# A Macaron encoder block on one core: output products in another order, an output projection by frame tile, norms without GpSimd

## The chip, the cores and the metric

The kernel runs on 1 core of one Trainium2 chip. The metric is the device time of one execution in microseconds, lower is better. A run gives one time; the figure used is the median of several runs of the same kernel.

## The reference

One streaming-encoder layer on 1024 frames of 1024 features, float32, with 256 memory tokens. `rms` is an RMS norm with a gain per feature.

```python
x  = x + 0.5 * rms(swiglu(rms(x, f1pre), ffn1_in, ffn1_out), f1post)   # D_FF 2816
h  = rms(x, mixpre)
q, k, v, g_out, f_low, p_in, xq, gates = split(h @ w_in)
a  = gated linear attention over 64-frame chunks (q, k, v, decay from f_low)
b  = trailing means of 2, 4, 8, 16 frames of p_in, a linear map per group
c  = cross-attention of xq into the normed memory
merged = sigmoid(gates) . (a @ w_up_gla, b @ w_up_pool, c @ w_up_xattn)
x  = x + rms(merged @ w_o, mixpost)
x  = x + 0.5 * rms(swiglu(rms(x, f2pre), ffn2_in, ffn2_out), f2post)
return rms(x, final_g)
```

## The kernel before, in words

**Tiles.** The frames are cut into 8 tiles of 128 (`NT`; `TPH` = 4 of them are a half). A matmul takes a 128x128 weight and 512 moving columns. For float32 accuracy each operand is split into a high and a low part (`acopy` on ScalarE writes the high one, `low` on VectorE subtracts it from the full one), and each product is three matmuls: low by high, high by low, high by high. Big arrays stand in 46 buffers of 128x1024 (`NB`, pool `bp`), all given out in one queue by first use; PSUM has 8 banks.

**Stages in order of time.** First norm and transposes; `ffn` for the first feed-forward part; its outputs are finished tile by tile by `finish1` (L923), which also makes the next norm and, by `turn2`, transposes the tile on TensorE; then keys, values, projections, attention, pooling and the three up-projections; then the output projection (L1385 to L1400); `ffn` again, finished by `finish2` and `last_norm` (L1408 on), which write the output.

**The output products of `ffn`** (L719 to L751). The second matrix product of the feed-forward part, 1024 frames by 2816 by 1024, is done with seven products of half size in place of eight (`out_product`, numbered 0 to 6). Each takes 11 steps of m, 4 frame tiles and 3 matmuls: 132 matmuls into 4 banks. By `by_rows` = 0 the steps run outermost, so all 4 tiles end together; by 2, two tiles are run through before the other two; by 1, tile after tile (33 matmuls each). The order before is 0, 4, 1, 5, 3, 2, 6. Product 2 completes frame tiles 0 to 3 and product 6 tiles 4 to 7, and each completed tile goes to `finish`.

**A norm** is `post_norm` (square and sum on ScalarE, a few 128x1 operations on VectorE for the inverse root, a product with the gain row, two `scalar_tensor_tensor` that scale and add the residual) and then `pre_norm` (the same for the next norm: product with the gain row, then a `tensor_scalar` by the inverse root). Its transposes are queued in `pending` and given out by `flush(keep)`.

**The output projection.** An outer loop over the two halves of the columns (`nh`), an inner one over the 8 tiles, 24 matmuls each; the norms of all tiles stand in the second half, after each tile's second group. `turn3` transposes a tile, splits it for tiles 0 to 3, and spills it to DRAM (`hfd`), from where `t_sums` fetches it again and forms the sums that the next `ffn` multiplies by. `between2` calls `t_sums` at j == 5 of the eight first products that `ffn` runs ahead.

**What orders the work.** Nothing is issued as it is written. A `Recorder` (class at L31) notes each operation with its engine, an estimated duration and what it depends on. `issue` (L188) then plays all of it through as a list schedule: an engine that is free takes the ready operation that was written first, a buffer is granted in the queue's order, and the sequence so found is fixed as each engine's instruction order. An operation with an `alt` may go to GpSimd (POOL) where that engine is free first: `tt` with `alt=True` (L149), used for the products with gain rows and for `low` of most weights.

```python
    def tt(self, o, a, b, op, alt=False):
        self.add("DVE", 0.07 + self.n(a) * 0.00104, [o], [a, b],
                 lambda: self.nc.vector.tensor_tensor(o, a, b, op=op),
                 alt=(0.1 + self.n(a) * 0.0022,
                      lambda: self.nc.gpsimd.tensor_tensor(o, a, b, op=op)) if alt else None)
```

In the trace all operations of one helper have one line: matmul L129, transpose L132, ScalarE's activation L146, VectorE's `tensor_tensor` L151 and its GpSimd alternative L153, `scalar_tensor_tensor` L162, `tensor_scalar` L168, `reciprocal` L171, DMA L186. So a place is told by its tiles: `ps` a PSUM bank, `b` a big buffer, `io` a residual tile, `g` a gain row, `s` the 128x1 scalars, `raw`/`wh`/`wl` a weight and its parts, `hh`/`hl` the parts of a transposed tile.

Of the kernel before, what the change touches and what calls it, by code (L numbers as in the profile page):

```python
# [35 lines left out]
class Recorder:  # L36
# [48 lines left out]
    def add(self, eng, dur, outs, ins, fn, table=None, alt=None):  # L85
# [31 lines left out]
        self.ops.append((eng, dur, deps, fn, table, alt))  # L117
# [16 lines left out]
    def act(self, o, i, func, scale=1.0, bias=0.0, accum_out=None):  # L134
# [9 lines left out]
        fixed = (0.052 if i.space == PSUM else 0.094) + (0.093 if accum_out is not None else 0.0)  # L144
# [14 lines left out]
    def stt(self, o, a, s, b, op0, op1):  # L159
        ins = [a, b] + ([] if isinstance(s, float) else [s])  # L160
        self.add("DVE", (0.07 if isinstance(s, float) else 0.13) + self.n(a) * 0.00104, [o], ins,
                 lambda: self.nc.vector.scalar_tensor_tensor(o, a, s, b, op0=op0, op1=op1))  # L162

    def ts(self, o, a, s1, s2, op0, op1=None):
        ins = [a] + [s for s in (s1, s2) if s is not None and not isinstance(s, (int, float))]
        kw = {} if op1 is None else {"op1": op1}
        self.add("DVE", (0.07 if len(ins) == 1 else 0.13) + self.n(a) * 0.00052, [o], ins,
                 lambda: self.nc.vector.tensor_scalar(o, a, s1, s2, op0=op0, **kw))  # L168

    def recip(self, o, a):  # L170
        self.add("DVE", 0.09, [o], [a], lambda: self.nc.vector.reciprocal(o, a))  # L171

    def reduce(self, o, a, axis, op):
        self.add("DVE", 0.07 + self.n(a) * 0.00105, [o], [a],
                 lambda: self.nc.vector.tensor_reduce(o, a, axis=axis, op=op))

    def vcopy(self, o, a):
        self.add("DVE", 0.07 + self.n(a) * 0.001, [o], [a], lambda: self.nc.vector.tensor_copy(o, a))

    def memset(self, o, v):  # L180
        self.add("DVE", 0.07 + self.n(o) * 0.001, [o], [], lambda: self.nc.vector.memset(o, v))
# [7 lines left out]
    def issue(self):  # L189
# [109 lines left out]
        for i in seq:  # L299
            ins = (ops[i][3] if ran[i] == ops[i][0] else ops[i][5][1])().ins  # L300
# [14 lines left out]
def block_kernel(  # L315
# [47 lines left out]
    def tt(o, a, b, op, alt=False):  # L363
        R.tt(o, a, b, op, alt)

    def low(o, full, high, alt=False):
        R.tt(o, full, high.bitcast(F32), op=ALU.subtract, alt=alt)
# [18 lines left out]
    def load_w(src, n=1024, alt=True):  # L386
# [3 lines left out]
        low(wl[:, :n], raw[:, :n], wh[:, :n], alt)  # L390
# [94 lines left out]
    def post_norm(y, gt, res, factor, table, alt=True):  # L485

        rs = row_rstd(y, factor, table)
        if alt:
            tt(y, y, gt, ALU.mult, alt=True)
        else:  # L490
            for i in range(2):
                cs = slice(i * 512, (i + 1) * 512)
                tt(y[:, cs], y[:, cs], gt[:, cs], ALU.mult)
# [111 lines left out]
    def ffn(win, wout, ops, between, finish, midway=None, ahead=6):  # L605
# [115 lines left out]
        ylo, yhi = y[:TPH], y[TPH:]  # L721
# [795 lines left out]
```

## Time and profile before

| | |
|---|---|
| median of 3 runs | 2380.36 us (2377.5 to 2385.82) |
| the profiled execution's own time | 2375.9 us |
| its span | 2374.1 us |
| mean granted TensorE clock | 0.984 |
| TensorE matmul busy | 2277.9 us, 96% |
| VectorE busy | 1556.9 us, 66% |
| ScalarE busy | 991.8 us, 42% |
| GpSimd busy | 125.1 us, 5% |

The table's busy times are over the whole span. A table by stretches of time gives for each stretch its length, the busy time of each engine with its instruction count, the granted clock and the DMA share. A list of waits says which engine's queue stood at which line, and on whose result. A timeline has one row for each instruction or run of equal ones: start, duration, engine, line, operation, output and inputs, and in brackets how long the engine had been idle and who released it. PE is TensorE, DVE VectorE, ACT ScalarE, POOL GpSimd.

### The profile page before, as it was taken

To read this page: it belongs to the slowest core of one execution; us is meant where nothing else is said; L and a number is where in the kernel's file an instruction comes from. 1 tells how busy PE (TensorE), PEld (TensorE's weight loads), DVE (VectorE), ACT (ScalarE), POOL (GpSimd) and SP (SyncE) were. 2 spreads that over 40 slices of the span, in tenths; PEclk is the share of its full clock that TensorE was granted. 3 is DMA by queue.
4 is the path that set the end of the run, shared out by engine and by line. 5 is a ranking of instruction groups with operands and counts; after the bars stand their busy time and mean duration, and the time that the engine had idled before them with its cause. 6 is when DMAs were issued, how large, how long until landed. Compare 5 with 4: busy or idle time off the path is not lost. (4 is left out here: it accounts for less than half of the span.)

```text
span 2374.1 us, 28161 instructions
## 1 busy us (share of the span) xinstructions
PE 2277.9 (96%) x10085; PEld 1843.9 (78%) x10085; DVE 1556.9 (66%) x2477; ACT 991.8 (42%) x1649; POOL 125.1 (5%) x53
## 2 busy tenths in 40 slices
PE   7999999999979999999999999999789999999996
PEld 6788888888768887777777788887668878888885
DVE  7887776754493545755666745553978877766448
ACT  7432333444356532366555542122543323345435
POOL 1000000000130002100000000001400000000002
PEclk8999999999999999999999999999999999999998
DMA  5346663676364632434444465341534666448553
GB/s 172 111 164 207 224 210 130 220 239 197 135 199 133 231 104 83 135 124 145 151 151 153 154 216 225 104 133 46 201 126 151 233 221 213 166 149 285 178 169 124
DMA packets 188477, 398.42 MB, mean 168 GB/s; under 512 B 19534, under 2 KB 50126, under 8 KB 188336
## 3 DMA queue, kind: packets, MB, share of 16 engines
q1 hardware_dynamic: 188336, 396.62, 50.0%
q8 instruction: 79, 1.29, 0.2%
q14 instruction: 62, 0.51, 0.1%
HBM read 273.34 MB, written 123.21 MB: 167 GB/s over the span
## 5 line engine op out<-in xcount | busy, mean ns | idle before, releaser
L129 PE MATMUL ps<-hl,wh 128*128 128x512 f32 (+1 forms) x1592 | 629.9, 396 | 14.7 <-ACT b L146 6.3
L129 PE MATMUL ps<-hh,wl 128*128 128x512 f32 (+1 forms) x1592 | 631.7, 397 | 6.5 <-DVE wl L151 6.5
L151 DVE TENSOR_TENSOR wl<-raw,wh 128x1024 fp32r<-128x1024 f32 x390 | 492.1, 1265 | 206.6 <-ACT wh L146 161.0
L146 ACT ACTIVATE wh<-raw 128x1024 fp32r<-128x1024 f32 x396 | 411.9, 1057 | 323.7 <-PE ps L129 150.2
L129 PE MATMUL ps<-hh,wh 128*128 128x512 f32 (+1 forms) x1592 | 427.9, 390 | 0.0
L129 PEld LDWEIGHTS ps<-hl,wh 128*128 128x128 f32 x1592 | 301.5, 189 | 91.8 <-issue 9.2
L129 PEld LDWEIGHTS ps<-hh,wl 128*128 128x128 f32 x1592 | 301.7, 190 | 68.2 <-DVE wl L151 7.8
L129 PEld LDWEIGHTS ps<-hh,wh 128*128 128x128 f32 x1592 | 299.2, 189 | 62.6 <-issue 0.7
L146 ACT ACTIVATE t<-ps 128x512 f32<-128x512 f32 x202 | 119.6, 597 | 417.3 <-PE ps L129 408.4
L129 PE MATMUL ps<-wl,wh 128*128 128x512 f32 x616 | 241.4, 392 | 4.6 <-DVE s L171 2.1
L129 PE MATMUL ps<-wh,wl 128*128 128x512 f32 x616 | 240.8, 391 | 0.0
L129 PE MATMUL ps<-wh 128*128 128x512 f32 x616 | 240.7, 391 | 0.0
L151 DVE TENSOR_TENSOR t<-ps,t 128x512 f32<-128x512 f32 x214 | 146.9, 687 | 137.5 <-PE ps L129 97.1
L146 ACT ACTIVATE b<-ps 128x512 f32<-128x512 f32 (+3 forms) x286 | 137.9, 496 | 192.6 <-PE ps L129 150.3
L129 PE MATMUL ps<-b,wh 128*128 128x512 f32 (+1 forms) x576 | 169.4, 377 | 0.0
L129 PE MATMUL ps<-hh,wq 128*128 128x512 f32 x528 | 165.7, 395 | 0.0
L153 POOL TENSOR_TENSOR b<-b,g 128x1024 f32<-128x1024 f32 x20 | 51.0, 2557 | 1967.3 <-ACT junk L146 1951.8
L151 DVE TENSOR_TENSOR raw<-raw,raw 128x512 f32<-128x512 f32 x176 | 122.6, 701 | 26.9 <-DMA raw<-in_ffn_out_dram 23.1
L129 PEld LDWEIGHTS ps<-wl,wh 128*128 128x128 f32 x616 | 116.5, 189 | 29.9 <-issue 3.3
L146 ACT ACTIVATE t<-t 128x512 f32<-128x512 f32 x98 | 61.8, 632 | 179.1 <-DVE t L151 178.9
L129 PEld LDWEIGHTS ps<-wh 128*128 128x128 f32 x616 | 116.3, 189 | 24.5
L129 PEld LDWEIGHTS ps<-wh,wl 128*128 128x128 f32 x616 | 116.4, 189 | 24.0
(104 smaller groups left out, 2635.6 us busy)
## 6 DMA issues: line engine op xcount, KB each, us to landing
raw<-in_ffn_in_dram SPq DMA_DIRECT2D x102, 512.0 KB, 4.0
raw<-actd SPq DMA_DIRECT2D x154, 256.0 KB, 3.0
actd<-b SPq DMA_DIRECT2D x88, 256.0 KB, 4.1
raw<-in_ffn_out_dram SPq DMA_DIRECT2D x44, 512.0 KB, 4.2
wsd<-raw SPq DMA_DIRECT2D x88, 256.0 KB, 2.9
raw<-wsd SPq DMA_DIRECT2D x88, 256.0 KB, 3.7
raw<-in_wfm_dram SPq DMA_DIRECT2D x44, 512.0 KB, 4.4
projd<-t SPq DMA_DIRECT2D x80, 256.0 KB, 2.8
```

The lines of the kernel that those rows point to most:

```text
L129: lambda: self.nc.tensor.matmul(o, l, r, start=first, stop=last, skip_group_check=more))
L146: lambda: self.nc.scalar.activation(o, i, func, **kw),
L151: lambda: self.nc.vector.tensor_tensor(o, a, b, op=op),
L153: lambda: self.nc.gpsimd.tensor_tensor(o, a, b, op=op)) if alt else None)
```

## The change

Six edits, in both feed-forward parts or around them:

- The GpSimd alternative is gone from `tt`, `low` and `load_w`; the ten GpSimd operations of the pooling stage (`pool_tt`) stay.
- `pre_norm` makes one `scalar_tensor_tensor` of its product and `tensor_scalar`.
- The estimated durations in the Recorder have larger fixed parts.
- The output products come in the order 0, 4, 3, 5, 2, 1, 6. Product 2 still completes tiles 0 to 3; products 1 and 6 follow. Product 0's result is copied to both halves' buffers, product 3 is read from PSUM twice and not copied, product 1 gets a bank of its own. `flush(2)` becomes `flush(1)`.
- The output projection takes one frame tile at a time: both column halves, then its norm. All 8 weight tiles of `wo` are loaded at the first tile.
- The weights of key group 0 are loaded within `finish1` at tile 4; `t_sums` of the second part is called at j == 3; `finish1` uses the square-root table for all tiles.

```diff
-    def tt(self, o, a, b, op, alt=False):
-        self.add("DVE", 0.07 + self.n(a) * 0.00104, [o], [a, b],
-                 lambda: self.nc.vector.tensor_tensor(o, a, b, op=op),
-                 alt=(0.1 + self.n(a) * 0.0022,
-                      lambda: self.nc.gpsimd.tensor_tensor(o, a, b, op=op)) if alt else None)
+    def tt(self, o, a, b, op):
+        self.add("DVE", 0.15 + self.n(a) * 0.00105, [o], [a, b],
+                 lambda: self.nc.vector.tensor_tensor(o, a, b, op=op))
...
-        self.add("DVE", (0.07 if isinstance(s, float) else 0.13) + self.n(a) * 0.00104, [o], ins,
+        self.add("DVE", 0.2 + self.n(a) * 0.00105, [o], ins,
...
-        fixed = (0.052 if i.space == PSUM else 0.094) + (0.093 if accum_out is not None else 0.0)
+        fixed = (0.17 if i.space == PSUM else 0.2) + (0.19 if accum_out is not None else 0.0)
...
     def pre_norm(src, n, gt, turn, table=False):
         rs = row_rstd(src, table=table)
-        tt(n, src, gt, ALU.mult, alt=True)
-        R.ts(n, n, rs, None, op0=ALU.mult)
+        R.stt(n, src, rs, gt, op0=ALU.mult, op1=ALU.mult)
...
         for t in range(TPH):
-            acopy(ylo[t][:, lo_], b1[t])
+            acopy(y2[t][:, lo_], b1[t])
+            acopy(y1[t][:, lo_], b1[t])
         b2 = [bank() for _ in range(TPH)]
         out_product(b2, 4, lambda m: wsd[1, m], False, 0)
         for t in range(TPH):
-            tt(yhi[t][:, hi_], b2[t], ylo[t][:, lo_], ALU.add)
-        out_product(b1, 1, lambda m: wout[2 * m + 1][:, lo_], True, 0)
-        for t in range(TPH):
-            acopy(yhi[t][:, lo_], b1[t])
-        out_product(b2, 5, lambda m: wsd[2, m], True, 0)
-        for t in range(TPH):
-            tt(ylo[t][:, hi_], b2[t], ylo[t][:, lo_], ALU.add)
+            tt(y1[t][:, hi_], b2[t], y1[t][:, lo_], ALU.add)
         b3 = [bank() for _ in range(TPH)]
         out_product(b3, 3, lambda m: wsd[0, m], False, 0)
         for t in range(TPH):
-            s5 = ttile()
-            acopy(s5, b3[t])
-            tt(ylo[t][:, hi_], ylo[t][:, hi_], s5, ALU.add)
+            tt(y1[t][:, hi_], b3[t], y1[t][:, hi_], ALU.add)
+        out_product(b2, 5, lambda m: wsd[2, m], True, 0)
+        for t in range(TPH):
+            tt(y2[t][:, hi_], b2[t], y2[t][:, lo_], ALU.add)
+            tt(y2[t][:, hi_], b3[t], y2[t][:, hi_], ALU.add)
         out_product(b2, 2, lambda m: wsd[3, m], True, 2)
         for t in range(TPH):
-            tt(ylo[t][:, lo_], b2[t], ylo[t][:, lo_], ALU.add)
-            finish(t, ylo[t])
-            flush(2)
-        out_product(b3, 6, lambda m: wout[2 * m + 1][:, hi_], True, 1)
+            tt(y2[t][:, lo_], b2[t], y2[t][:, lo_], ALU.add)
+            finish(t, y2[t])
+            flush(1)
+        b1 = [bank() for _ in range(TPH)]
+        out_product(b1, 1, lambda m: wout[2 * m + 1][:, lo_], False, 0)
         for t in range(TPH):
-            tt(yhi[t][:, hi_], b3[t], yhi[t][:, hi_], ALU.add)
-            finish(t + TPH, yhi[t])
-            flush(2)
+            tt(y1[t][:, lo_], b1[t], y1[t][:, lo_], ALU.add)
+        b3 = [bank() for _ in range(TPH)]
+        out_product(b3, 6, lambda m: wout[2 * m + 1][:, hi_], False, 1)
+        for t in range(TPH):
+            tt(y1[t][:, hi_], b3[t], y1[t][:, hi_], ALU.add)
+            finish(t + TPH, y1[t])
+            flush(1)
...
-    z = [btile() for _ in range(NT)]
-    for nh in range(2):
-        ws = [load_w(wo[nh, kk], alt=False) for kk in range(4)]
-        for t in range(NT):
-            cs = slice((t % TPH) * P, (t % TPH + 1) * P)
+    ws = {}
+    for t in range(NT):
+        z = btile()
+        cs = slice((t % TPH) * P, (t % TPH + 1) * P)
+        for nh in range(2):
+            if t == 0:
+                ws[nh] = [load_w(wo[nh, kk]) for kk in range(4)]
+            w = ws[nh]
...
     def between2(j):
         flush()
-        if j == 5:
+        if j == 3:
```

**TensorE's order at the end of the first feed-forward part.** In the fences a number behind a name is that buffer's own; `ps_608` is a bank of product 2's second pair of tiles, `b_560` and `b_561` are frame tiles 0 and 1 after their norms, and `ps_708` (before) is a bank of product 6, `ps_768` (after) one of product 1. Before:

```order
L129 MATMUL ps_608_701<-wh_780_873,wl_781_874 128x512
L129 MATMUL ps_608_701<-wh_780_873 128x512
L132 MATMUL ps_794_887<-ident_73,b_560_653 128x128 x4
L132 MATMUL ps_795_888<-ident_73,b_560_653 128x128 x4
L132 MATMUL ps_800_893<-ident_73,b_561_654 128x128 x4
L132 MATMUL ps_801_894<-ident_73,b_561_654 128x128 x4
L129 MATMUL ps_708_801<-wl_804_897,wh_803_896 128x512
```

Of the changed kernel:

```order
L129 MATMUL ps_608_701<-wh_743_836,wl_744_837 128x512
L129 MATMUL ps_608_701<-wh_743_836 128x512
L132 MATMUL ps_754_847<-ident_73,b_560_653 128x128 x4
L132 MATMUL ps_755_848<-ident_73,b_560_653 128x128 x4
L129 MATMUL ps_768_861<-wl_774_867,wh_773_866 128x512
L129 MATMUL ps_768_861<-wh_773_866,wl_774_867 128x512
```

Before, two tiles' transposes stand between product 2 and the last product; now one tile's stand there, and product 1 comes in front of product 6.

**VectorE's order for one tile of the output projection**: `io` is the residual tile, `b` the tile itself, `g` the gain row of the next norm, `s` the scalars. Before:

```order
L162 SCALAR_TENSOR_TENSOR io_2144<-b_2103,s_2145,io_2144 128x512 x2
L151 TENSOR_TENSOR b_2103<-io_2144,g_2094 128x1024
...
L168 TENSOR_SCALAR s_2146<-s_2146 128x1 x3
L168 TENSOR_SCALAR s_2149<-s_2149 128x1
L162 SCALAR_TENSOR_TENSOR s_2146<-s_2146 128x1
...
L168 TENSOR_SCALAR b_2103<-b_2103,s_2146 128x1024
```

Of the changed kernel:

```order
L151 TENSOR_TENSOR b_2107<-b_2107,g_2097 128x1024
L166 TENSOR_SCALAR s_2135<-s_2135 128x1 x2
L160 SCALAR_TENSOR_TENSOR s_2135<-s_2135 128x1 x5
...
L160 SCALAR_TENSOR_TENSOR io_2134<-b_2107,s_2135,io_2134 128x512 x2
...
L160 SCALAR_TENSOR_TENSOR b_2107<-io_2134,s_2136,g_2098 128x1024
```

The first norm's product with the gain row now stands in VectorE's queue (before it was on GpSimd's), the second norm's product and scaling are one instruction, and a tile's scalars no longer alternate with those of the next tile.

**TensorE's order at the end of the output projection**: `ps_2115`, `ps_2120`, `ps_2124` are banks of the second feed-forward part's first products; `b_2017` (before) and `b_2098` (after) are frame tile 7. Before:

```order
L132 MATMUL ps_2101_2194<-ident_73,b_2016_2109 128x128 x4
L132 MATMUL ps_2102_2195<-ident_73,b_2016_2109 128x128 x4
L129 MATMUL ps_2115_2208<-hh_2008_2101,wl_2114_2207 128x512
...
L132 MATMUL ps_2109_2202<-ident_73,b_2017_2110 128x128 x4
L132 MATMUL ps_2110_2203<-ident_73,b_2017_2110 128x128 x4
L129 MATMUL ps_2115_2208<-hh_2008_2101,wh_2113_2206 128x512
```

Of the changed kernel:

```order
L129 MATMUL ps_2124_2217<-hl_2013_2106,wh_2122_2215 128x512
L132 MATMUL ps_2113_2206<-ident_73,b_2098_2191 128x128 x4
L132 MATMUL ps_2114_2207<-ident_73,b_2098_2191 128x128 x4
L129 MATMUL ps_2124_2217<-hh_2012_2105,wl_2123_2216 128x512
```

Between the projection's last matmul and tile 7's transposes stand 62 of the next part's matmuls before and 73 now; behind the transposes, up to the first matmul that needs the sums of `t_sums`, 130 before and 119 now.

## Rows read from the trace of the kernel before

**Rows 1.** Busy time by stage: stretch, length, each engine's busy us (instructions), clock, DMA.

```profile
core 0: us, PE busy (x) PEld busy (x) DVE busy (x) ACT busy (x) POOL busy (x), PEclk, DMA share, GB/s
0.00:76.00 76.00, 57.41 (x254) 45.32 (x255) 61.68 (x150) 51.68 (x123) 7.29 (x7) 0.82 0.41 141
...
613.00:720.00 107.00, 87.91 (x373) 71.51 (x372) 87.23 (x179) 56.33 (x139) 36.91 (x14) 0.89 0.52 170
...
1650.00:1760.00 110.00, 84.31 (x383) 66.31 (x382) 95.92 (x221) 60.22 (x120) 28.36 (x10) 0.98 0.52 172
1760.00:1900.00 140.00, 140.00 (x619) 115.95 (x618) 117.27 (x167) 44.31 (x58) 0.00 (x0) 1.00 0.54 181
1900.00:1960.00 60.00, 56.65 (x240) 45.69 (x239) 47.26 (x69) 17.42 (x24) 0.00 (x0) 0.97 0.64 222
```

**Rows 2.** The same view, cut to four spells of half clock.

```profile
645.80:652.60 6.80, 4.89 (x20) 4.45 (x21) 6.33 (x15) 4.38 (x13) 2.33 (x1) 0.50 0.90 289
666.20:673.00 6.80, 5.11 (x13) 3.86 (x13) 6.33 (x13) 0.20 (x1) 0.68 (x1) 0.50 0.88 293
697.00:700.40 3.40, 2.74 (x9) 2.35 (x10) 3.22 (x11) 0.29 (x2) 0.00 (x0) 0.50 0.78 213
710.60:717.40 6.80, 5.33 (x17) 4.59 (x18) 5.73 (x20) 3.61 (x9) 0.55 (x1) 0.50 0.62 192
```

**Rows 3.** TensorE's waits, 598 to 720 us: us in total, times, longest.

```profile
PE ps L132 <- DVE s L162: 5.4, 1, 5.4
...
PE ps L132 <- DVE b L151: 2.7, 1, 2.7
PE ps L129 <- DVE s L171: 2.1, 1, 2.1
PE ps L132 <- DVE b L168: 1.9, 1, 1.9
```

**Rows 4.** GpSimd's groups by form: busy us, mean ns, idle time before.

```profile
L153 POOL TENSOR_TENSOR b<-b,g 128x1024 f32<-128x1024 f32 x20 | 51.0, 2557 | 1967.3 <-ACT junk L146 1951.8 <-DMA b<-in_x_dram 15.5
L153 POOL TENSOR_TENSOR b<-io,g 128x1024 f32<-128x1024 f32 x13 | 36.4, 2800 | 57.0 <-DVE io L162 25.2 <-issue 16.8 <-DVE s L162 12.2
L153 POOL TENSOR_TENSOR wl<-raw,wh 128x1024 fp32r<-128x1024 f32 x6 | 15.7, 2624 | 111.4 <-ACT dec L146 73.1 <-ACT wh L146 38.4
```

**Rows 5.** VectorE's groups by form, 1600 to 1760 us.

```profile
L162 DVE SCALAR_TENSOR_TENSOR s<-s 128x1 f32<-128x1 f32 x80 | 23.9, 325 | 0.6
L151 DVE TENSOR_TENSOR wl<-raw,wh 128x1024 fp32r<-128x1024 f32 x9 | 14.8, 1647 | 0.0
...
L162 DVE SCALAR_TENSOR_TENSOR io<-b,s,io 128x512 f32<-128x512 f32 x16 | 11.5, 747 | 0.3
...
L151 DVE TENSOR_TENSOR b<-io,g 128x1024 f32<-128x1024 f32 x5 | 6.1, 1225 | 0.1
```

**Rows 6.** Timeline, 1640 to 1664 us: GpSimd, then VectorE.

```profile
1649.80 2.38 POOL L153 TENSOR_TENSOR b<-b,g 128x1024 f32<-128x1024 f32 x1 [4.82 <-ACT junk L146]
...
1649.89 2.31 DVE L162 SCALAR_TENSOR_TENSOR s<-s 128x1 f32<-128x1 f32 x1
...
1652.23 0.16 DVE L162 SCALAR_TENSOR_TENSOR s<-s 128x1 f32<-128x1 f32 x1
...
1653.60 0.75 DVE L168 TENSOR_SCALAR b<-b,s 128x1024 f32<-128x1024 f32 x1
...
1657.55 0.42 DVE L151 TENSOR_TENSOR hl<-ps,hh 128x256 fp32r<-128x256 f32 x1
```

**Rows 7.** Busy time, cut at tile 7's transposes in the output projection.

```profile
1592.00:1720.30 128.30, 110.51 (x504) 90.08 (x503) 80.56 (x217) 52.80 (x123) 30.96 (x11) 0.99 0.40 135
...
1721.30:1757.70 36.40, 28.56 (x119) 21.44 (x117) 25.18 (x24) 19.28 (x27) 0.00 (x0) 1.00 0.44 140
```

**Rows 8.** Timeline at the end: TensorE's last matmul, VectorE's last two adds.

```profile
2353.07 0.39 PE L129 MATMUL ps<-wh 128*128 128x512 f32 x1
...
2354.52 0.67 DVE L151 TENSOR_TENSOR b<-ps,b 128x512 f32<-128x512 f32 x1
...
2362.32 0.69 DVE L151 TENSOR_TENSOR b<-ps,b 128x512 f32<-128x512 f32 x1
```

More of the change, by code (lines that the diff above doesn't have):

```diff
@@ L83, in _region, with add @@
         return name, m, (p0, p0 + pn)
-    def add(self, eng, dur, outs, ins, fn, table=None, alt=None):
+    def add(self, eng, dur, outs, ins, fn, table=None):
         idx = len(self.ops)
@@ L116, in add @@
         deps.discard(idx)
-        self.ops.append((eng, dur, deps, fn, table, alt))
+        self.ops.append((eng, dur, deps, fn, table))
     @staticmethod
@@ L166, in ts @@
         kw = {} if op1 is None else {"op1": op1}
-        self.add("DVE", (0.07 if len(ins) == 1 else 0.13) + self.n(a) * 0.00052, [o], ins,
+        self.add("DVE", (0.15 if len(ins) == 1 else 0.2) + self.n(a) * 0.00052, [o], ins,
                  lambda: self.nc.vector.tensor_scalar(o, a, s1, s2, op0=op0, **kw))
     def recip(self, o, a):
-        self.add("DVE", 0.09, [o], [a], lambda: self.nc.vector.reciprocal(o, a))
+        self.add("DVE", 0.15, [o], [a], lambda: self.nc.vector.reciprocal(o, a))
     def reduce(self, o, a, axis, op):
-        self.add("DVE", 0.07 + self.n(a) * 0.00105, [o], [a],
+        self.add("DVE", 0.15 + self.n(a) * 0.00105, [o], [a],
                  lambda: self.nc.vector.tensor_reduce(o, a, axis=axis, op=op))
     def vcopy(self, o, a):
-        self.add("DVE", 0.07 + self.n(a) * 0.001, [o], [a], lambda: self.nc.vector.tensor_copy(o, a))
+        self.add("DVE", 0.15 + self.n(a) * 0.001, [o], [a], lambda: self.nc.vector.tensor_copy(o, a))
     def memset(self, o, v):
-        self.add("DVE", 0.07 + self.n(o) * 0.001, [o], [], lambda: self.nc.vector.memset(o, v))
+        self.add("DVE", 0.15 + self.n(o) * 0.001, [o], [], lambda: self.nc.vector.memset(o, v))
     def dma(self, o, i):
@@ L253, in issue @@
                     i = heapq.heappop(ready[e])
-                    if ran[i]:
-                        continue
-                    dur = ops[i][1] if e == ops[i][0] else ops[i][5][0]
+                    dur = ops[i][1]
                     if ops[i][4] not in (None, table):
@@ L299, in issue @@
         for i in seq:
-            ins = (ops[i][3] if ran[i] == ops[i][0] else ops[i][5][1])().ins
+            ins = ops[i][3]().ins
             done_by[i] = ins.name
@@ L361, in acopy, with tt, low @@
             R.act(o, i, AF.Copy, scale=scale)
[L363 to L367, printed above, removed]
+    def tt(o, a, b, op):
+        R.tt(o, a, b, op)
+    def low(o, full, high):
+        R.tt(o, full, high.bitcast(F32), op=ALU.subtract)
     def mm(o, l, r, first, last, more=False):
@@ L384, in load_raw, with load_w @@
         return raw
-    def load_w(src, n=1024, alt=True):
+    def load_w(src, n=1024):
         raw = load_raw(src, n)
@@ L483, in flush, with post_norm @@
             pending.pop(0)()
-    def post_norm(y, gt, res, factor, table, alt=True):
+    def post_norm(y, gt, res, factor, table, parts=1):
         rs = row_rstd(y, factor, table)
[L488 to L493, printed above, removed]
+        for i in range(parts):
+            cs = slice(i * D // parts, (i + 1) * D // parts)
+            tt(y[:, cs], y[:, cs], gt[:, cs], ALU.mult)
         for i in range(2):
@@ L924, in into @@
             tuple(a.rearrange("p (k c) -> p k c", k=2) for a in (hh, hl)))
+    kv0 = []
     def finish1(t, yt):
@@ L931, in finish1 @@
         R.dma(xt, x[t * P:(t + 1) * P, :])
-        post_norm(yt, gains["post"], xt, 0.5, t < 6)
+        post_norm(yt, gains["post"], xt, 0.5, True)
         R.dma(x1d[t], xt)
-        pre_norm(xt, yt, gains["pre"], lambda n: turn2(n, t), t < 6)
+        pre_norm(xt, yt, gains["pre"], lambda n: turn2(n, t), True)
+        if t == TPH:
+            kv0.extend(load_w(wkv[0, kk]) for kk in range(4))
         if t >= TPH:
@@ L961, in fetch, with kv_group @@
         return b
-    def kv_group(g):
-        ws = [load_w(wkv[g, kk]) for kk in range(4)]
+    def kv_group(g, ws=None):
+        if ws is None:
+            ws = [load_w(wkv[g, kk]) for kk in range(4)]
         for pr in range(4):
@@ L1326, in side @@
         yield
-    run(chain(kv_group(0), kv_group(1)), side())
+    run(chain(kv_group(0, kv0), kv_group(1)), side())
     hops.update(B11=hm[0][0:2], B21=hm[0][2:4], B22=hm[1][2:4])
@@ L1383, in turn3 @@
         spill(f, t)
-    z = [btile() for _ in range(NT)]
-    for nh in range(2):
-        ws = [load_w(wo[nh, kk], alt=False) for kk in range(4)]
-        for t in range(NT):
-            cs = slice((t % TPH) * P, (t % TPH + 1) * P)
+    ws = {}
[6 more added lines that the diff above has]
+            w = ws[nh]
             ps = bank()
             mm3(ps, [(mh[t // TPH][k // 2][:, k % 2, cs], ml[t // TPH][k // 2][:, k % 2, cs],
-                      ws[k // 2][0][:, (k % 2) * 512:(k % 2 + 1) * 512],
-                      ws[k // 2][1][:, (k % 2) * 512:(k % 2 + 1) * 512]) for k in range(KD)])
-            acopy(z[t][:, nh * 512:(nh + 1) * 512], ps)
-            if nh == 1:
-                xt = R.tile(bp, [P, 1024], F32, "b", nm("io"), NB)
-                R.dma(xt, x1d[t])
-                post_norm(z[t], gains["mpost"], xt, 1.0, False)
-                R.dma(x2d[t], xt)
-                pre_norm(xt, z[t], gains["f2pre"], lambda n, t=t: turn3(n, t))
-                flush(1)
+                      w[k // 2][0][:, (k % 2) * 512:(k % 2 + 1) * 512],
+                      w[k // 2][1][:, (k % 2) * 512:(k % 2 + 1) * 512]) for k in range(KD)])
+            acopy(z[:, nh * 512:(nh + 1) * 512], ps)
+        xt = R.tile(bp, [P, 1024], F32, "b", nm("io"), NB)
+        R.dma(xt, x1d[t])
+        post_norm(z, gains["mpost"], xt, 1.0, False)
+        R.dma(x2d[t], xt)
+        pre_norm(xt, z, gains["f2pre"], lambda n, t=t: turn3(n, t))
+        flush(1)
     def between2(j):
         flush()
-        if j == 5:
+        if j == 3:
             t_sums(h3, True)
```

18 lines of the change are left out of this document (8 added, 10 removed).

## The prediction

> **What bounds the kernel now.** The table by stages comes first [rows 1]. Between 1760 and 1900 us TensorE is busy 140.00 of 140 us with 619 matmuls, so 0.226 us each; most of the span looks like this, and there nothing is to be had but fewer matmuls, and their number does not change. Time can go only where TensorE stands: 18.6 of 76 us at the start, 19.1 of 107 us between 613 and 720 (107 - 87.91; stage A, where the first feed-forward part ends and its tiles are normed), 25.7 of 110 us between 1650 and 1760 (stage B, the output projection and the entry into the second part), 3.4 of 60 us at 1900, and the tail behind the last matmul. Stage A pays twice: in four spells the granted clock is 0.50, so 1.2 in place of 2.4 GHz, and in each TensorE is busy only 72 to 81% of the time [rows 2]. TensorE's busy time in the four is 4.89 + 5.11 + 2.74 + 5.33 = 18.07 us; at full clock it would be half, so 9.0 us went there. Stage A lost 19.1 + 9.0 = 28.1 us.
>
> Next the list of waits [rows 3]: in stage A TensorE stands for VectorE, mostly at transposes (L132) that wait for a tile's norm. VectorE is busy 87.23 of those 107 us and 95.92 of 110 in stage B [rows 1], so it paces both, while between 1900 and 1960 it has slack. These are also the stages in which GpSimd works, 36.91 and 28.36 us. Its groups are 20 + 13 products with a gain row and 6 weight splits [rows 4], all alternatives of VectorE's work, 2.56 to 2.80 us each where VectorE takes 1.225 [rows 5]. The timeline shows what they do to VectorE [rows 6]: GpSimd starts at 1649.80 for 2.38 us, VectorE's 128x1 operation starts at 1649.89 and takes 2.31 us; the same form takes 0.16 us at 1652.23. The reader sees an instruction of one column held for as long as GpSimd runs.
>
> **The change, part by part.** *GpSimd's work goes to VectorE.* 39 instructions: 14 in stage A [rows 1], 11 in B [rows 7], 7 in the tail, 7 elsewhere. Added on VectorE at 1.225 us: 17.2 in A, 13.5 in B, 8.6 in the tail. Given back is the hold. In 1600 to 1760 us two forms show it [rows 5]: 80 one-column operations at 325 ns in place of 160 lose 13.2 us, 9 weight splits at 1647 in place of 1225 lose 3.8. That is 17.0 us of GpSimd's 30.96 [rows 7], a share of 0.55; other forms lose some too, and I take 0.6. The ends are 0.55 and 1 (all of GpSimd's time). At 0.6 stage A gets back 22.1, B 18.6.
>
> The Trainium skill, SBUF — State Buffer, section "Who interferes with whom", says that the ports are an exclusive lock: whoever comes second waits for the whole instruction. If every GpSimd instruction held VectorE so, all 36.91 us of stage A would come back, and stage A could then give all of its 28.1 us. The rows bear out the lock but not the share, since an instruction that reads PSUM ran its 0.42 us at 1657.55; I keep 0.6.
>
> *`pre_norm` as one instruction.* It removes 0.75 us (1653.60, [rows 6]) and the product of 1.225 and adds a `scalar_tensor_tensor` of 1024 columns, which no row shows. Bounds: the 1.225 of a product of that size, and two of 512 columns at 747 ns, 1.49 [rows 5]. So 0.5 to 0.75 us saved per tile, 0.6 taken: 5 us in each stage of 8 tiles. VectorE's load falls by 22.1 - 17.2 + 5 = 10 us in A and by 18.6 - 13.5 + 5 = 10 in B.
>
> *The product order, stage A.* Tiles 0 to 3 are completed before product 1 and not before the last product, so one product earlier: 132 x 0.226 = 29.9 us. Four norms and their transposes now lie beside products 1 and 6 (59.8 us of TensorE), where before they met the other four. What stays: tiles 4 to 7 still end one row of 33 matmuls (7.5 us) apart with the last product, and their transposes come last; product 1 wants banks that the first tile's transposes also want; product 6's rows need weight splits that stand among norms in VectorE's queue. I leave three of the seven waits, 2.7 + 2.1 + 1.9 = 6.7 us [rows 3], and one half-clock spell, 5.11 / 2 = 2.6 [rows 2]: 9.3 of 28.1 remain, **18.8 us gained**. The ends are 5 and 28. The second copy of product 0's result lies on ScalarE, which is busy 56.33 of 107 us here, and is costed at nothing; so is the copy of product 3 that goes. The four weight loads of key group 0 pass SP's queue earlier beside a DMA share of 0.52 [rows 1], also at nothing; uncovered they would delay weights of product 6 by a few us, which the upper end holds.
>
> *The output projection by tile, stage B.* The first matmul is at 1592.00. Up to tile 7's transposes TensorE has 384 matmuls (86.8 us), 62 of the next part (14.0), and 56 transposes of other tiles, at 0.82 us for 8 some 6 us: 106.8 us, but it takes 128.3 [rows 7], of which 17.8 are idle. Before, all norms stand in the second half of this; by tile, each norm has 48 matmuls (10.8 us) and a transpose beside it. VectorE needs for a tile some 20 scalar operations (3.5 us), 1.225 + 1.49 + 1.4 for the wide ones and 4 splits of 0.42, so about 9 us: it keeps up, if buffers come free in time. Then tile 7's transposes stand at 1592 + 106.8 + 11 x 0.226 = 1701.3, 19.0 us earlier. Behind them the chain is the same: spill, fetch, sums, first matmul on them, 36.4 us [rows 7]. Of this TensorE covers 28.56 now; with 11 matmuls fewer 26.1, so it stands 10.3 us and not 7.8. That costs no time of its own, since the chain sets the end, but one longer stand may cost a half-clock spell, again 2.6 us. **16.4 us gained**; ends 12 and 19. On SP's queue the last spill is followed by four fetches and then weight loads, where one weight load stood between; nothing is costed for that.
>
> *The tail.* The last matmul ends at 2353.46; VectorE's add of that tile's result starts at 2362.32, 8.9 us late, since the queue of earlier tiles is in front of it [rows 8]. From there 11.8 us to the span's end stay. With tiles 0 to 3 done a product earlier and no hold, the backlog has 59.8 us to vanish in; tile 6's own work (about 7 us) fits into the last row of 7.5 us. I leave one matmul's 0.4 us: **8.5 gained**, ends 5 and 9.
>
> *At nothing*: three products at the start go to VectorE, 3.7 us for 0.6 x 7.29 = 4.4 returned, beside DMA waits; the new estimated durations reorder queues where TensorE hardly stands; square roots by table for two tiles.
>
> The sum: 18.8 + 16.4 + 8.5 = 43.7 us. The profiled execution took 2375.9, so 2332.2; it lies 4.5 us under the median of 2380.36, on which the forecast is put: 2380.4 - 43.7 = **2336.7**. With all ends together the forecast's own case runs from 2324 (28 + 19 + 9) to 2358 (5 + 12 + 5); most of it lies between 2326 and 2346.
>
> **The rivals.**
> *Stage A is not gained.* Products 1 and 6 now have to share VectorE and the 8 banks with the norms; product 1 takes four banks while the transposes of tiles 0 to 3 want two at a time. For it: of the waits one stands at a matmul of a product (L129), not at a transpose [rows 3], so products are held up too. Against it: VectorE's load falls. If stage A gives 5 us: 2380.4 - 5 - 16.4 - 8.5 = 2350.5. Chance 0.12.
> *Stage B is not gained.* The 16 weight tiles of `wo`, 16 merged tiles, 8 parts of h and 2 gain rows are 42 of the 46 buffers, so tile, residual and transposed tile have four, and a tile's norm may wait for the spill of the one ahead. Then tile 7 comes when it came, 0 to 5 us gained: 2380.4 - 18.8 - 2.5 - 8.5 = 2350.6. For it: the buffers' count; against it: 17.8 us of idle time that need not be there. Chance 0.10.
> *New waits in the bodies eat the gain.* Another order of products and other durations reorder some 1,300 us in which TensorE runs without a gap. At 1900 to 1960 there is one such wait, 3.4 us and a half-clock spell that costs 1.7 (clock 0.97 of 60 us, [rows 1]). Eight of these, one at each of the four products that change place in both parts, cost 41 us: 2378, no change. Chance 0.05.
> *Slower: the hold is not GpSimd's.* If VectorE's long instructions have another cause, the 32 instructions of A, B and tail are pure load: 17.2 - 5 in A, 13.5 - 5 in B, 8.6 in the tail, 29 us on the engine that paces these stages. No order of products helps then, and 2380.4 + 29 = 2409. It decides from where less than half of the share of 0.6 comes back. Against it: [rows 6]. The Trainium skill, Perfetto Trace Analysis, section "Optimizing Scalar/DVE Operations", has the rule that work may go to GpSimd where VectorE is saturated, though the shared port may spoil it; by the first half of it this change is wrong. Chance 0.05.
> That the change does not do what it says is excluded: in the order GpSimd's queue is down to the ten operations of the pooling stage.
>
> **How the numbers follow.** The forecast has the remaining 0.68. A measurement tells about 0.3%, 7 us, from no change. Faster: 0.68 + 0.12 + 0.10 = 0.90; the same 0.05; slower 0.05. The range reaches from 2318 (all of the lower ends, and a few us more should the full hold come back) to 2360, which takes in both rivals of one stage lost; left out are the last two cases and some of the edges.
>
> **What would show it.** In the profile after: VectorE's one-column operations in stages A and B at 160 to 220 ns; no GpSimd work outside the pooling stage; TensorE idle about 7 and not 19 us at the end of the first part, tile 7's transposes about 109 us behind the projection's first matmul, then a stand of some 10 us; the last add within 1 us of the last matmul and 12 us from the end. It is wrong if TensorE waits for weight splits (`wl`) inside products 1 and 6, if the projection's matmuls wait for buffers, or if the bodies of the two parts lose more than 5 us.

## The result, and the profile after

The changed kernel takes 2312.86 us (median of 4 runs, 2312.55 to 2313.34), the kernel before 2379.96 beside it: a ratio of 0.9715 (95% interval 0.9697 to 0.9733), 67 us less. The forecast was 2336.7, in a range from 2318 to 2360; the measured time lies 5 us below that range. The profiled execution's span fell from 2374.1 to 2310.8, by 63.3 us; the profiled execution of the kernel before lies 4.1 us under its median.

The table of stretches of the changed kernel answers to [rows 1]: stage A is now 613 to 700 us, stage B 1568.4 to 1720.

```profile
0.00:76.00 76.00, 54.65 (x247) 41.49 (x247) 59.77 (x152) 52.00 (x124) 0.20 (x4) 0.86 0.39 134
...
613.00:700.00 87.00, 82.21 (x381) 67.45 (x380) 71.99 (x148) 54.05 (x123) 0.00 (x0) 0.98 0.74 239
...
1626.00:1678.30 52.30, 52.30 (x248) 43.62 (x247) 34.66 (x107) 27.22 (x59) 0.00 (x0) 1.00 0.51 168
1678.30:1720.00 41.70, 35.08 (x152) 27.21 (x151) 35.11 (x36) 26.42 (x33) 0.00 (x0) 1.00 0.41 139
...
1860.00:1960.00 100.00, 100.00 (x443) 82.81 (x442) 80.46 (x116) 32.14 (x42) 0.00 (x0) 1.00 0.64 217
```

TensorE stands 4.8 us in stage A where it stood 19.1, not at all in the projection up to tile 7's transposes, then 6.6 of 41.7 us, and not at all from 1860 to 1960. The list of its waits in 598 to 720 us has one wait of a transpose left, beside 0.9 us for weight splits; [rows 3] is from a list of seven waits, four of them at transposes:

```profile
PE ps L132 <- DVE b L160: 3.9, 1, 3.9
```

VectorE's groups by form in 1568 to 1700 us, beside [rows 5]: the one-column operations are at 193 ns where they were at 325, the weight splits at 1220 where they were at 1647.

```profile
L160 DVE SCALAR_TENSOR_TENSOR s<-s 128x1 f32<-128x1 f32 x80 | 15.4, 193 | 2.0
...
L151 DVE TENSOR_TENSOR wl<-raw,wh 128x1024 fp32r<-128x1024 f32 x9 | 11.0, 1220 | 8.5 <-ACT wh L146 8.5
L160 DVE SCALAR_TENSOR_TENSOR b<-io,s,g 128x1024 f32<-128x1024 f32 x8 | 10.3, 1283 | 0.1
```

The end, beside [rows 8]: VectorE's last add starts as the last matmul ends, and the span ends 11.2 us later.

```profile
2299.21 0.39 PE L129 MATMUL ps<-wh 128*128 128x512 f32 x1
```

```profile
2299.63 0.69 DVE L151 TENSOR_TENSOR b<-ps,b 128x512 f32<-128x512 f32 x1 [1.18 <-PE ps L129]
```

To compare kernels the span is cut at matmuls that all of them have: the first of the first part's output products; the last of the up-projections, from which stage B runs to tile 7's transposes; the last of the second part's first layers; the last of all. In us of the profiled execution ("A on" is from the first output product to the projection; "behind" from tile 7's transposes to the last first-layer matmul):

| kernel | time | ratio to before | A on | B | behind | tail |
|---|---|---|---|---|---|---|
| before | 2380.0 | | 1128.2 | 129.3 | 421.4 | 20.7 |
| changed | 2312.9 | 0.9715 (0.9697 to 0.9733) | 1103.9 | 110.8 | 409.6 | 11.2 |
| e1 | 2346.0 | 0.9861 (0.9846 to 0.9876) | 1112.6 | 116.9 | 425.9 | 11.2 |
| e2 | 2376.6 | 0.9991 (0.9981 to 1.0000) | 1131.6 | 129.6 | 420.3 | 14.5 |
| e3 | 2360.3 | 0.9927 (0.9907 to 0.9947) | 1128.5 | 111.6 | 418.6 | 20.4 |
| e4 | 2370.8 | 0.9968 (0.9955 to 0.9981) | 1126.8 | 129.4 | 417.1 | 15.0 |
| e5 | 2317.2 | 0.9744 (0.9729 to 0.9758) | 1106.2 | 110.8 | 409.3 | 13.1 |
| e6 | 2333.4 | 0.9810 (0.9796 to 0.9825) | 1104.8 | 120.0 | 420.9 | 11.2 |
| e7 | 2327.2 | 0.9789 (0.9773 to 0.9806) | 1108.1 | 104.5 | 426.2 | 11.6 |
| e8 | 2325.8 | 0.9782 (0.9768 to 0.9797) | 1109.6 | 108.4 | 419.7 | 12.1 |
| e9 | 2317.5 | 0.9743 (0.9729 to 0.9758) | 1104.1 | 110.2 | 415.7 | 11.2 |
| e10 | 2324.6 | 0.9774 (0.9759 to 0.9788) | 1109.3 | 105.2 | 422.2 | 11.5 |
| e11 | 2328.1 | 0.9788 (0.9773 to 0.9802) | 1107.1 | 109.5 | 421.6 | 11.2 |
| e13 | 2345.2 | 0.9854 (0.9839 to 0.9869) | 1111.3 | 115.7 | 426.2 | 11.7 |

The cuts of e2 and e3 are from executions 4.3 and 2.6 us under their medians. From the last first-layer matmul to the last matmul every kernel takes 211.0 us, except e4 with 215.6. B and behind are best read as a sum, since a kernel that moves the next part's matmuls ahead of tile 7 lengthens one and shortens the other.

### The profile page after: what moved, and what is told of

It reads as the page before. It is cut to its first block, busy times and chain, and to the rows that moved or that the text cites. A ratio compares the mean times of both kernels' runs of the same rounds, so it can differ in the third digit from the quotient of the medians.

```text
span 2310.8 us, 28033 instructions
## 1 busy us (share of the span) xinstructions
PE 2262.8 (98%) x10085; PEld 1840.6 (80%) x10085; DVE 1541.5 (67%) x2496; ACT 990.4 (43%) x1645; POOL 22.9 (1%) x14
## 4 chain that ended last, share of the span: by engine, by line
PE 91%; DVE 4%; DMA 2%; issue 1%; ACT 1%; SPq 0%; DVEq 0%; ACTq 0%
PE ps L129 89%; PE ps L132 1%; DVE wl L151 1%; DMA raw<-in_ffn_out_dram 1%; DVE b L151 1%; DVE hl L151 1%; DMA b<-vd 1%; DVE raw L151 0%; DMA b<-projd 0%; ACT b L146 0%; ACT junk L146 0%; DVE t L151 0%; DMA raw<-in_ffn_in_dram 0%; ACT wh L146 0%; ACT hh L146 0%
## 5 line engine op out<-in xcount | busy, mean ns | idle before, releaser
L129 PE MATMUL ps<-hh,wl 128*128 128x512 f32 (+1 forms) x1592 | 625.2, 393 | 3.3 <-DVE wl L151 3.3
L151 DVE TENSOR_TENSOR wl<-raw,wh 128x1024 fp32r<-128x1024 f32 x396 | 481.3, 1224 | 188.7 <-ACT wh L146 119.6
L129 PE MATMUL ps<-hh,wh 128*128 128x512 f32 (+1 forms) x1592 | 434.8, 392 | 0.0
L146 ACT ACTIVATE t<-ps 128x512 f32<-128x512 f32 x194 | 114.7, 597 | 371.4 <-PE ps L129 354.6
L146 ACT ACTIVATE b<-ps 128x512 f32<-128x512 f32 (+4 forms) x286 | 137.1, 497 | 206.3 <-PE ps L129 176.3
L151 DVE TENSOR_TENSOR raw<-raw 128x512 f32<-128x512 f32 x176 | 120.5, 687 | 7.9 <-DMA raw<-in_ffn_out_dram 5.4
```

The lines of the kernel that those rows point to most:

```text
L129: lambda: self.nc.tensor.matmul(o, l, r, start=first, stop=last, skip_group_check=more))
L146: lambda: self.nc.scalar.activation(o, i, func, **kw),
L151: lambda: self.nc.vector.tensor_tensor(o, a, b, op=op))
```

## The experiments

**One part alone, on the kernel before.** e1 puts all alternatives on VectorE:

```diff
-                 alt=(0.1 + self.n(a) * 0.0022,
-                      lambda: self.nc.gpsimd.tensor_tensor(o, a, b, op=op)) if alt else None)
+                 alt=None)
```

> The kernel before with its 39 GpSimd alternatives put on VectorE and nothing else changed. Theory H (the hold of VectorE by GpSimd is what makes stages A and B late): one-column operations fall to 160 to 220 ns, and stage A, stage B and the tail each give 8 us or more, so 2355 us or less. Theory O (the order of the work makes them late, GpSimd only uses slack): VectorE's load falls, but norms still come in a heap, so within 10 us of before, 2370 to 2385. If the hold is not GpSimd's: 2400 or more.

Measured 2346.0: 15.6 us less from A on, 7.9 in B and behind (550.7 to 542.8), 9.5 in the tail. Up to tile 7's transposes it is 12.4 us shorter; 4.5 are lost again behind them, where TensorE waits 10.7 us in one piece for a weight split. One-column operations in 1600 to 1760 us are at 189 ns. The busy row of its page:

```profile
PE 2272.5 (97%) x10085; PEld 1840.2 (79%) x10085; DVE 1530.3 (65%) x2516; ACT 992.1 (42%) x1649; POOL 22.0 (1%) x14
```

VectorE took over 39 instructions (39 x 1.225 = 47.8 us) and is busy 26.6 us less than before (1556.9). So 74.4 us had been hold, 0.72 of the 103.1 us that GpSimd worked less. The hold is GpSimd's; Theory H stands in stage A, up to tile 7's transposes and in the tail.

Not every form is held. In 1600 to 1760 us the kernel before has, beside the forms of [rows 5],

```profile
L151 DVE TENSOR_TENSOR s<-s 128x1 f32<-128x1 f32 x16 | 6.8, 427 | 0.2
L151 DVE TENSOR_TENSOR hl<-ps,hh 128x256 fp32r<-128x256 f32 x16 | 6.5, 417 | 0.4 <-ACT hh L146 0.2
L168 DVE TENSOR_SCALAR s<-s 128x1 f32<-128x1 f32 x32 | 5.4, 177 | 45.4 <-ACT junk L146 45.2
```

and e1

```profile
L151 DVE TENSOR_TENSOR hl<-ps,hh 128x256 fp32r<-128x256 f32 x16 | 6.5, 414 | 0.2
L167 DVE TENSOR_SCALAR s<-s 128x1 f32<-128x1 f32 x32 | 5.6, 176 | 45.4 <-ACT junk L146 45.2
L151 DVE TENSOR_TENSOR s<-s 128x1 f32<-128x1 f32 x16 | 2.4, 153 | 0.1
```

so the one-column `tensor_tensor` was held, the one-column `tensor_scalar` and the split that reads PSUM were not. The single instructions of the kernel before say the same: of those that overlap one of GpSimd's 39, 14 one-column `scalar_tensor_tensor` take 1658 ns on average (195 elsewhere) and 6 one-column `tensor_tensor` 2098 (154), but 32 one-column `tensor_scalar` take 197 (170 elsewhere) and 20 splits that read PSUM 414 (417).

e2 has only the block of output products of the change's diff (`y = ...` to `flush(1)`).

> The kernel before with the new order of the output products alone; GpSimd keeps its work. Theory O: stage A gains 15 us or more and the tail 5 or more, 2360 us or less, with one-column operations still at 300 to 400 ns on average. Theory H: the held VectorE stays the pace of stage A, under 8 us gained, 2372 or more.

Measured 2376.6, 2 us less by the ratio and not clear of no change. Stage A itself (to the first matmul with `wf`, behind the norms) shortens by 4.0 us, but what follows it, up to the output projection, takes 7.4 us longer; that the heap of norms moved there is argued, not shown. The tail gains 6.2. With VectorE held, the order is worth nothing clear of the noise.

e3 has only the projection's loops of that diff (`ws = {}` and on; `wo` loaded without GpSimd, as before).

> The kernel before with the output projection taken by frame tile, alone. Theory O: tile 7's transposes come 15 us or more earlier and the chain behind them gets shorter too, by some 7 us, since no heap of spills stands in front of the last one: 2358 us or less. Theory H: VectorE is held still and needs more than the 10.9 us of a tile, under 8 us gained, 2372 or more.

Measured 2360.3, between the two theories and nearer to O: B and behind 20.5 us shorter, 17.7 of it before tile 7's transposes. Here the order pays without GpSimd's removal, against Theory H.

e4 has only the estimated durations:

```diff
-        self.add("DVE", 0.07 + self.n(a) * 0.00104, [o], [a, b],
+        self.add("DVE", 0.15 + self.n(a) * 0.00105, [o], [a, b],
...
```

> The kernel before with the Recorder's new estimated durations alone; the GpSimd alternatives stay. Theories H and O both: queues shuffle a little, within 7 us of before. A third theory (the estimates order the queues so that waits go, in stage A and in the bodies): 2365 us or less, and the wait of 2 us and half-clock spell at 1902 us gone.

Measured 2370.8, 7.6 us faster by the ratio, at the edge of what both theories gave and short of the third's 2365. By the cuts the tail gives 5.7 us and the stretch behind tile 7 gives 4.3, though it has a wait of 11.1 us for a weight split; the last output products lose 4.6, by a wait of 2.7 us and a half-clock spell at 2329.6. The wait of the second part's body is gone, as the third theory had it. Of TensorE's waits in 1850 to 1950 us the kernel before has this row, e4 none:

```profile
PE ps L129 <- DVE t L151: 2.8, 2, 2.1
```

A wait of this kind stands in that part's body in every kernel with the old estimates (before, e1, e2, e3, e7, e10, e13) and, but for one of 0.7 us in e12, in none with the new.

**One part undone, in the changed kernel.** e5 has the block of output products, e6 the projection's loops, e7 the estimates with the signs of the change's diff reversed. e8 gives the alternative back to two products:

```diff
-            tt(y[:, cs], y[:, cs], gt[:, cs], ALU.mult)
+            tt(y[:, cs], y[:, cs], gt[:, cs], ALU.mult, alt=parts == 1)
...
-            tt(yt[:, cs], xt[:, cs], gains2["fin"][:, cs], ALU.mult)
+            tt(yt[:, cs], xt[:, cs], gains2["fin"][:, cs], ALU.mult, alt=t < NT - 1)
```

> The changed kernel with the output products in the old order (0, 4, 1, 5, 3, 2, 6; flush(2)), all else as changed. By the runs so far the order alone was worth 4 us in stage A and 6 in the tail with GpSimd at work, and 7 us were lost again between the stages. Theory H (GpSimd's hold was the cause, the order is worth little without it): within 7 us of the changed kernel, 2312 to 2320. Theory O (the order pays once VectorE is free): stage A longer by 8 us or more, 2322 or more.

> The changed kernel with the output projection in the old form (column halves outermost, all norms in the second half), all else as changed. Theory O: the stretch to tile 7's transposes grows from 110.8 us towards the 116.9 that it had without GpSimd, and the next stretch loses its gain as well: 2325 us or more. Theory H: within 7 us, 2320 or less.

> The changed kernel with the old estimated durations. If the gain in the second feed-forward part (421 to 410 us behind tile 7's transposes) comes of the estimates, as the 417 us of the run with the new estimates alone suggests, this run is 4 to 10 us slower than the changed kernel, 2317 to 2323, with the wait near the part's end back. If it comes of the projection by tile or of the missing GpSimd work: within 3 us.

> The changed kernel with the GpSimd alternative given back to the product with the gain row in post_norm and last_norm only; weight splits and pre_norm stay on VectorE. Theory H: each GpSimd product of 2.4 us holds VectorE again; stage A, stage B and the tail lose 4 to 9 us each, 2325 to 2340. Theory O: VectorE has room in the new order, so within 7 us of the changed kernel.

e5: 2317.2, only 4 us slower. The order of the products is a minor part, 2.3 us from A on (5.7 in stage A itself, 3.4 of them lost behind it) and 1.9 in the tail. e6: 2333.4, 20 us slower, as large as alone; three transposes wait 4.8, 3.5 and 3.1 us again. e7: 2327.2, 14 us slower, more than any theory had; the body's wait is back, and a stand of 7.4 us behind tile 7. e8: 2325.8, 13 us slower. GpSimd works 60.3 us more (83.2 against 22.9) and takes 23 products from VectorE, 28.2 us, yet VectorE is busy 17.7 us longer: 45.9 of the 60.3 us are hold, 0.76. Of the time lost, 5.7 us are from A on and 10.1 behind tile 7, where one wait for a weight split is 8.2 us; how much of that wait is hold and how much a shifted queue, no run separates.

**The gain behind tile 7.** e7 and e8 both brought back one long stand there. e9 calls `t_sums` later again, nothing else.

```diff
-        if j == 3:
+        if j == 5:
             t_sums(h3, True)
```

> The changed kernel with t_sums called at j == 5 as before, all else as changed. Theory S (the chain behind tile 7 is shorter because weight splits of the next pairs come ahead of the sums in VectorE's queue, and that place is given by the call): the stretch from tile 7's transposes to the last first-layer matmul, 410 us, grows by 5 us or more, 2318 or more. Theory P (it is shorter because tile 7's spill stands alone on SP's queue, with no heap of earlier tiles): no change by over 3 us.

Measured 2317.5, half a microsecond short of Theory S's 2318, and 6.1 us longer behind tile 7: Theory S. VectorE's timeline in e9, then TensorE's:

```profile
1686.88 3.76 DVE L151 TENSOR_TENSOR b<-b,b 128x1024 f32<-128x1024 f32 x3 [11.93 <-DMA b<-hfd]
...
1706.45 1.22 DVE L151 TENSOR_TENSOR wl<-raw,wh 128x1024 fp32r<-128x1024 f32 x1
```

```profile
1707.72 0.79 PE L129 MATMUL ps<-hh,wl 128*128 128x512 f32 x1 [8.76 <-DVE wl L151]
```

VectorE stands 11.93 us for the first sum's data with no split ahead of it; the next split comes behind the sums, and TensorE waits for it 8.76 us in one piece. In the changed kernel two splits stand in that gap, ahead of the first sum:

```profile
1681.03 1.23 DVE L151 TENSOR_TENSOR wl<-raw,wh 128x1024 fp32r<-128x1024 f32 x1 [4.78 <-ACT wh L146]
1683.48 1.22 DVE L151 TENSOR_TENSOR wl<-raw,wh 128x1024 fp32r<-128x1024 f32 x1 [1.23 <-ACT wh L146]
1686.24 1.23 DVE L151 TENSOR_TENSOR b<-b,b 128x1024 f32<-128x1024 f32 x1 [1.53 <-DMA b<-hfd]
```

and TensorE's stands there are of 1.9 us at most. Theory P's half is true of the chain and not of the gain. In the kernel before the first sum was

```profile
1731.80 1.23 DVE L151 TENSOR_TENSOR b<-b,b 128x1024 f32<-128x1024 f32 x1 [11.76 <-DMA b<-hfd]
```

11.5 us behind the start of tile 7's transposes (1720.3); in the changed kernel it is 7.9 us behind them (1678.3), in e9 8.6. So e9 has most of the shorter way through DRAM and still loses the 6.1 us.

e10 has the three named parts on the kernel before (edits of e1, e2, e3).

> The kernel before with three parts: no GpSimd alternatives, the new product order, the projection by tile; old estimates, pre_norm in two instructions, t_sums at j == 5, weights of key group 0 late. If these three are the change: within 7 us of the changed kernel, 2320 or less. If the estimates and the small edits carry what the run with old estimates lost (14 us): 2325 to 2335.

Measured 2324.6: 12 us of the 67 are in the estimates and small edits. Of the small edits the earlier weights of key group 0 and the square-root table were not run alone. Its span is 14.2 us longer than the changed kernel's, 5.4 of it from A on and 7.0 in B and behind.

e11 writes `pre_norm` in two instructions again; e13 fuses it in e1's kernel.

```diff
-        R.stt(n, src, rs, gt, op0=ALU.mult, op1=ALU.mult)
+        tt(n, src, gt, ALU.mult)
+        R.ts(n, n, rs, None, op0=ALU.mult)
```

> The changed kernel with pre_norm as a product and a tensor_scalar again. VectorE gets some 0.6 us more per tile. If VectorE is no longer the pace: within 3 us of the changed kernel. If it still is at the last tiles: stage A's one wait of 3.9 us grows by 1 to 3 us, and the time by up to 6 us.

> The kernel before without GpSimd alternatives and with pre_norm in one instruction. Beside the run without alternatives (2346.0). Theory L (the 15 us that the split pre_norm cost in the changed kernel are VectorE's load at the last tiles): stages A and B each shorter by 3 to 6 us, 2334 to 2341. Theory F (they are one long stand of TensorE that a shifted queue brings back, and could as well have gone the other way): within 3 us, or the gain lies in one stand alone.

e11: 2328.1, 15 us slower, far above both expectations; 12.0 of it behind tile 7. e13: 2345.2, no gain over 2346.0 (stage A is 3.0 us shorter, the start 2.7 longer). So it is mostly Theory F: the same edit is worth 15 us or 1, and 12 of the 15 go with a long stand, which in e1 and e13 is there either way. Behind tile 7 TensorE's waits for a weight split are these, of e11, e13 and e1 in turn (in us: total, times, longest; in the changed kernel the longest is 1.9):

```profile
PE ps L129 <- DVE wl L151: 7.8, 1, 7.8
```

```profile
PE ps L129 <- DVE wl L151: 11.1, 1, 11.1
```

```profile
PE ps L129 <- DVE wl L151: 11.6, 2, 10.7
```

**What is left.** The largest remaining stand of the changed kernel is at 67 to 76 us, for weights of the first pair. e16 runs one more first product ahead in each part (e12 the same kernel, alone: 2306.9, ratio 0.9700), e14 two; e15 is the changed kernel beside them. The edit of e14 (e16 has 7 and 9 in place of 8 and 10):

```diff
-    def ffn(win, wout, ops, between, finish, midway=None, ahead=6):
+    def ffn(win, wout, ops, between, finish, midway=None, ahead=8):
...
-            flush(5 - j)
+            flush(max(0, 5 - j))
...
-    ffn(f2in, f2out, h3, between2, finish2, ahead=8)
+    ffn(f2in, f2out, h3, between2, finish2, ahead=10)
```

> The changed kernel with one more first product ahead in each feed-forward part (7 and 9 in place of 6 and 8; flush(5 - j) kept at 0 or more). What is left in it at 67 to 76 us (7.4 us and a half-clock spell) and behind tile 7's transposes (some 6 us) are stands of TensorE for weights, and one more pair is 24 matmuls, 5.4 us. If that work fits into the stands: 5 to 10 us faster than the changed kernel, 2303 to 2308. If the added weight loads and splits only push the others back: within 3 us, or slower.

> The changed kernel with two more first products ahead in each feed-forward part (8 and 10). If the stands left at 74 and 1685 to 1694 us are still stands for work: 2 to 4 us faster than with one more ahead, 2303 to 2305. If the buffers are used up by then: the same as with one, or slower.

> The changed kernel itself, beside the next on the same chip: 2311 to 2315 us by every theory.

> The changed kernel with one more first product ahead in each part (7 and 9), again, beside the changed kernel on the same chip: 5 to 7 us faster than it, as the runs apart had it.

On one chip: e15 2313.0 (2311.7 to 2313.5), e16 2305.9 (2304.5 to 2307.5), e14 2301.3 (2298.4 to 2303.2; ratio to before 0.9671, 0.9656 to 0.9685). e14 beats the kernel before and the changed one, the latter by 11.7 us; the first output product starts at 454.9 and not 464.3. Its first stretch:

```profile
0.00:76.00 76.00, 61.81 (x282) 48.46 (x282) 60.84 (x151) 53.88 (x127) 0.20 (x4) 0.89 0.43 148
```

35 more matmuls fit in the first 76 us, against the changed kernel's row above: the stands were room for work, as far as two more pairs reach.

## Why the prediction was wrong

The direction and the stages were right, the size was not: 43.7 us in the sum, 63.3 in the span. Cut at the table's marks, the 19.6 missing are spread as the points below say; the second is no stretch of its own, its gain lies within the others. For the first, the sums of the stretch from tile 7's transposes to the last first-layer matmul, before (421.4 - 409.3 = 12.1 us idle) and after:

```profile
sum 421.40, PE 409.30 PEld 334.22 DVE 324.37 ACT 146.89 POOL 0.00; mean PE 102.33 PEld 83.55 DVE 81.09 ACT 36.72 POOL 0.00
```

```profile
sum 409.60, PE 402.98 PEld 331.73 DVE 325.57 ACT 150.39 POOL 0.00; mean PE 134.33 PEld 110.58 DVE 108.52 ACT 50.13 POOL 0.00
```

- **"Behind them the chain is the same", 14.4 us.** This is the step that failed. The text let the chain of 36.4 us stand, expected TensorE to stand 10.3 us in it and priced that at -2.6. It gained 11.8. TensorE stands 6.6 us from tile 7's transposes to the end of the first layers, where it stood 12.1 before (5.5); 11 matmuls had gone ahead (2.5); the half-clock spell at 1905 is gone (1.7); 2.1 are not placed. Taking the chain as a fixed length that ends TensorE's wait was the error. Its first sum comes 3.6 us sooner, and TensorE does not stand once for its end but in six pieces, for a weight split (3.3 us) or for ScalarE (3.3). Where the splits stand in VectorE's queue is worth 6.1 us by the place of one call (e9), and 12.0 by `pre_norm` (e11).
- **"New estimated durations ... at nothing".** Alone they gave 7.6 us, undone 14. Where "TensorE hardly stands" there were waits of 3.35 us with a half-clock spell to be had, and behind tile 7 an order of splits to be lost (e7's stand of 7.4 us); alone, they also took 5.7 us from the tail (e4).
- **Stage A, 18.8 said, 22.0 found, 3.2 us.** The size is near and the reason wrong. The text gave it to the product order, with VectorE's load lower; e1 has 14.6 of it (255.8 to 241.2 us) from GpSimd's removal alone, while the order alone made 4.0 of it and nothing of the whole (e2), and in the changed kernel is worth 5.7 of it and 4 of the whole (e5). GpSimd's work was counted as load on VectorE, 10 us lighter, and not as time of the waits, though the hold falls on the one-column operations of a norm, and the longest wait of a transpose in [rows 3], 5.4 us, is for one.
- **B up to tile 7, 19.0 said, 18.5 found**, and e3 shows that the loops did it: 17.7 alone. TensorE does not stand there at all, so buffers were no limit and that rival falls.
- **The tail, 8.5 said, 9.5 found.** The cause given does not single itself out: e1 has all of it without the new order, e2 6.2 without e1, and e4 5.7 with neither.
- 2.3 us in the middle and -0.7 at the start, both costed at nothing.

The share of the hold, 0.6 by two forms, is 0.72 over the kernel (e1) and 0.76 in e8. Two forms that were left out, 16 one-column `tensor_tensor` at 427 in place of 153 ns and 8 wide `tensor_scalar` at 1010 in place of 747, lose another 6.5 us in [rows 5]'s window. The row at 1657.55, from which the prediction argued for a smaller share, shows nothing: GpSimd's product of 1649.80 had ended at 1652.18, and the next is

```profile
1660.34 2.37 POOL L153 TENSOR_TENSOR b<-b,g 128x1024 f32<-128x1024 f32 x1 [8.16 <-ACT junk L146]
```

That the form which reads PSUM is not held is so all the same: 20 such splits that do overlap GpSimd take 414 ns (under e1). The Trainium skill's exclusive lock (SBUF — State Buffer, "Who interferes with whom") agrees in kind with the 2.31 us of a one-column operation beside GpSimd's 2.38; by all of GpSimd's time stage A would have given all of its 28.1 us, and it gave 22.0. The Trainium skill's other rule (Perfetto Trace Analysis, "Optimizing Scalar/DVE Operations") is that work may go to GpSimd where VectorE is saturated, with the warning that the shared port may spoil it. The warning is what holds here: taking such work away gained 33 us by the ratio (e1), giving 23 products back lost 13 (e8).

The lower end of the range, 2318, added up the ends of the costed terms. The estimates and the stretches put at nothing had no end at all, and for the stretch behind tile 7 the best end was no loss.

## What to carry to other kernels

Look first at what a helping engine does to the engine it helps: 39 instructions moved to GpSimd cost VectorE 74 us where they saved it 48. In a kernel whose order is fixed from estimated durations, an edit in one place can move instructions in others, so a term "at nothing" needs bounds like the others, and an edit's worth is measured in the kernel it goes into: `pre_norm` in one instruction was worth 1 us in one kernel and 15 in the other. A queue that is in order can hide work in a wait, if that work stands ahead of the waiting instruction.

## What the runs showed of the hardware

A long stand of TensorE cost more than its own length. In e9 TensorE stands from 1698.96 to 1707.72, and the granted clock is 0.50 (1.2 of 2.4 GHz) from 1702.0 to 1712.2. The changed kernel's TensorE stands 6.2 us within 22, in pieces of at most 1.9, and the clock stays at 1.00. The stretches of e9, then of the changed kernel:

```profile
1702.00:1712.20 10.20, 4.47 (x11) 3.51 (x12) 10.10 (x11) 2.11 (x2) 0.00 (x0) 0.50 0.27 71
```

```profile
1690.00:1712.00 22.00, 15.84 (x65) 11.49 (x64) 21.90 (x22) 14.27 (x19) 0.00 (x0) 1.00 0.26 86
```

The length of one stand does not decide it alone: in e1 a stand of 1.87 us that ends at 1897.33 is followed by a clock of 0.50 from 1898.2 to 1901.6, and before one of 2.05 us that ends at 1904.29 by the same from 1905.3 to 1908.7.

GpSimd's `tensor_tensor` held some of VectorE's forms and not others (under e1): beside it a one-column `scalar_tensor_tensor` took 1658 ns on average where the others took 195, a one-column `tensor_scalar` 197 where the others took 170, and a split that reads PSUM 414 where the others took 417.

A `scalar_tensor_tensor` of 1024 columns takes 1283 ns, close to the lower of the bounds set for it (1225 and 1490).
